# Feed-forward of a hybrid decoder layer: the second product's first raw operands on memory of the first product's last units, loaded by GpSimd's queue

## The chip, the cores and the metric

The kernel runs on one core of one Trainium2 chip. The metric is the device time of one execution in microseconds (us). The core has a tensor engine (TensorE, PE, with its weight loads as PEld), three engines for elementwise work (VectorE or DVE, ScalarE or ACT, GpSimd or POOL), and queues through which transfers between HBM and the on-chip memory are issued. In this kernel nearly all transfers are issued by SyncE (SP), a few by GpSimd.

## The reference

The layer computes attention and a state-space branch, merges them, and then runs a dense feed-forward network. Only the last part matters here:

```python
h = h + merged @ w_out[i]
hn = rmsnorm(h, norm_ffn[i])
gate, up = jnp.split(hn @ w_ffn_in[i], 2, axis=-1)
h = h + (jax.nn.silu(gate) * up) @ w_ffn_out[i]
return h[:, N_META:]
```

`h` is 1024 x 1024 in float32, `w_ffn_in` is 1024 x 5632 and `w_ffn_out` 2816 x 1024.

## The kernel before

All large products are exact to float32: each operand is split into a high and a low part (`hi` by a cast on ScalarE, `lo` by a subtraction on VectorE or GpSimd), and three matmuls (high-high, high-low, low-high, `PASSES`) take the place of one. On top of it the feed-forward network uses a scheme of seven products for a 2 x 2 block product instead of eight. The products are called "11", "12", "2", "3", "1", "22" and "4", in the order in which they run (`ORDER`), and their operands are sums and differences of quarters.

*First product.* For each even j of 0 to 20, `ffn_unit` computes a gate unit `fg{j}` and an up unit `fu{j}`; `fg20` and `fu20` are the last. Their activations' halves are in the X tiles (`Xt..`, `Xb..`), which stay on chip for the whole first product. `finish` (L1163) multiplies silu(gate) by up, makes the sums a1, a2, c12 (the operand "3") and a4 on GpSimd, and stores the seven results to `act_d` in HBM by SP (L1179).

*Second product.* `ffn_out(j0, n, last)` runs four times, with (j0, n) = (0,2), (2,3), (5,3), (8,3). Each stage loads seven raw A operands of `act_d` (`rawa`, L1206; 512 KB each where n is 2) and two raw weight tiles of `w_ffn_out` (`rawb`, L1211; 1 MB each where n is 2). `rawb0_0` holds b11 and b12, `rawb0_1` b21 and b22. VectorE makes t1 = b12 - b11, t2 = b22 - t1, t3 = b22 - b12 and t4 = b21 - t2, which are the B operands of products "1", "2", "3" and "22". `operand` (L1225) splits: the high half on ScalarE (L1228), the low half on VectorE for A and on GpSimd for B (L911, a helper that all elementwise sums share). Each product has four groups (one per row block b) of n x 3 matmuls of 128x128 by 128x512: 24 matmuls where n is 2, 36 where n is 3. The results are in PSUM banks `ch` and `si`; VectorE adds each of them to the residual tiles `h2o0` to `h2o7` (L911). `h2o` is loaded once, in stage j0=0, by 16 loads of 256 KB (L1198). Products "11", "2", "1", "4" share the banks `ch`, so product "2" can only write a bank after VectorE has added it to h2o.

*What sets the order.* Every engine and every queue runs its instructions in order. The order itself is set by a scheduler when the program is built, from its own model of the times, and instructions wait for each other by semaphores. Tiles come from pools; two tiles that lie on the same memory make the later one's writer wait for the earlier one's last reader. Before, the raw tiles lie where the X tiles were, so SP's first raw load (`rawa11_0`) waits for the last matmul of product "4" of `fu20`, and all loads behind it wait too.

Of the kernel before, what the change touches and what calls it, by code (L numbers as in the profile page):

```python
# [8 lines left out]
F32 = mybir.dt.float32  # L9
F32R = mybir.dt.float32r  # L10
# [7 lines left out]
P = 128  # L18
# [28 lines left out]
def hybrid_layer_kernel(ctx: ExitStack, tc: tile.TileContext, x, meta_tokens, norm_mix, w_in, q_norm, k_norm,  # L47
                        attn_sinks, lam_re, lam_im, log_dt, ssm_b_re, ssm_b_im, ssm_c_re, ssm_c_im, ssm_d,
                        w_glu, attn_branch_norm, ssm_branch_norm, w_out, norm_ffn, w_ffn_in, w_ffn_out, out):
    nc = tc.nc  # L50
    x, out = x[0], out[0]
    w_in, w_glu, w_out, w_ffn_in, w_ffn_out = w_in[0], w_glu[0], w_out[0], w_ffn_in[0], w_ffn_out[0]

    def sbuf(name, bufs, side="left"):
        return tc.tile_pool(name=name, bufs=bufs, side=side, reuse_waits="tile")
# [15 lines left out]
    pool_w = front.enter_context(sbuf("pool_w", 8))  # L71
    pool_r = front.enter_context(sbuf("pool_r", 2))
# [156 lines left out]
    with sbuf("p1", 2) as p1:  # L229
# [147 lines left out]
        fr, fi, den, nr = sm("fr"), sm("fi"), sm("den"), sm("nr")  # L377
# [542 lines left out]
    def parts_of(t):  # L920
        return [t[:, p].rearrange("p (k n) -> p k n", k=4) for p in range(2)]

    early = {}
    with sbuf("op", 2) as op_:
# [32 lines left out]
                    nc.tensor.transpose(pt[:, k * P:(k + 1) * P], v[:, k * P:(k + 1) * P], ident)  # L957
                split(*(X[key][p][:, :, c:c + P] for p in range(2)), pt.rearrange("p (k n) -> p k n", k=4))

        for key in ("b11", "b21", "b22"):  # L960
            x_part(key, pool_x)
        for n in range(2):
            w = w_cols(w_out, n * 512, 512, f"o{n}", nc.vector)
# [115 lines left out]
        mixed("t4", "b21", "t2", ALU.subtract)  # L1079
    big_cm.__exit__(None, None, None)  # L1080

    with sbuf("fp", 2) as fp:
        turn_w = [0]

        def operand(src, name):

            turn_w[0] += 1
            pool = fp if turn_w[0] % 3 == 0 else pool_w
            t = parts_of(pool.tile([P, 2, 512], F32R, tag="w", **({"bufs": 4} if pool is fp else {}), name=name))
            split(*t, src)  # L1090
            return t

# [26 lines left out]
        def ffn_unit(c0, u, name):  # L1119


            a = w_quarters(c0, [(pool_r, fp)[u % 2]] * 2, name)
            ops = {}

            def s_(key, x_, y_, op):
                t = fp.tile([P, 512], F32, tag="sum", name=f"s{key}_{name}")
                t = t.rearrange("p (k n) -> p k n", k=4)
                tt_(t, x_, y_, op)
                return t
            ops["11"] = operand(a["11"], f"w11_{name}")  # L1130
            ops["12"] = operand(a["12"], f"w12_{name}")
            s1 = s_("1", a["21"], a["22"], ALU.add)
            s2 = s_("2", s1, a["11"], ALU.subtract)
            ops["2"] = operand(s2, f"w2_{name}")
            ops["1"] = operand(s1, f"w1_{name}")
            ops["4"] = operand(s_("4", a["12"], s2, ALU.subtract), f"w4_{name}")
            ops["3"] = operand(s_("3", a["11"], a["21"], ALU.subtract), f"w3_{name}")
            ops["22"] = operand(a["22"], f"w22_{name}")

            chain, side, third = bank(f"ch_{name}", "m"), bank(f"si_{name}", "s"), bank(f"th_{name}", "x")  # L1140
            banks[u] = {"11": chain, "12": side, "2": chain, "3": third, "1": chain, "22": third, "4": chain}
            c = {}
            for key in ORDER:
                step_(u, ops, key, key in FIRST, name)
                if key == "11":
                    c["11"] = cell(f"c11_{name}")
                    nc.scalar.copy(c["11"], chain)
                elif key == "12":
                    tt_(c["11"], c["11"], side, ALU.add)
                elif key == "2":  # L1150
                    c["21"] = cell(f"c21_{name}")
                    nc.scalar.copy(c["21"], chain)
                elif key == "3":
                    c["22"] = cell(f"c22_{name}")
                    nc.scalar.copy(c["22"], third)
                elif key == "1":
                    tt_(c["22"], c["22"], chain, ALU.add)
                elif key == "22":
                    tt_(c["21"], c["21"], third, ALU.add)
            c["12"] = chain  # L1160
            return c
# [21 lines left out]
                     [ffn_unit(i * DFF + j * P, j + i, f"f{'gu'[i]}{j}") for i in range(2)]), j)  # L1183


    front.close()
    with (sbuf("fo", 16) as fo, sbuf("rw", 2) as rw, sbuf("ra", 4) as ra, sbuf("fh", 8) as fh,
          sbuf("fs", 3) as fs):
        h2 = [fh.tile([P, D], F32, tag="h", name=f"h2o{b}") for b in range(8)]
        QUARTER = {q: (int(q[0]) - 1, int(q[1]) - 1) for q in ("11", "12", "21", "22")}  # L1190
# [3 lines left out]
        def load_h2(q):  # L1194
            r, cc = QUARTER[q]
            for b in range(4 * r, 4 * r + 4):
                cols = slice(512 * cc, 512 * cc + 512)
                nc.sync.dma_start(out=h2[b][:, cols], in_=h2_d[b][:, cols])  # L1198

        def ffn_out(j0, n, last):  # L1200
# [2 lines left out]

            def load_a(q):
                t = ra.tile([P, G, 512], F32, tag="raw", name=f"rawa{q}_{j0}")[:, :n]
                nc.sync.dma_start(out=t, in_=act_d[q][j0:j0 + n].rearrange("j p n -> p j n"))  # L1206
                raw["a" + q] = t

            def load_b(i):
                t = rw.tile([P, G, D], F32, tag="raw", name=f"rawb{j0}_{i}")[:, :n]  # L1210
                nc.sync.dma_start(out=t, in_=w2[i][:, j0:j0 + n, :])  # L1211
                for h in range(2):
                    raw[f"b{i + 1}{h + 1}"] = t[:, :, 512 * h:512 * h + 512]
            for i, q in enumerate(("11", "12", "2", "1", "3", "22", "4")):
                load_a(q)
                if i < 2:
                    load_b(i)
                if not j0 and i < 4:
                    load_h2(("11", "21", "22", "12")[i])

            def s_(key, x_, y_, op):
                t = fs.tile([P, G, 512], F32, tag="sum", name=f"{key}_{j0}")[:, :n]
# [73 lines left out]
```

## Time and profile before

| | us |
|---|---|
| median of 3 runs | 1692.15 (1691.48 to 1692.57) |
| the profiled execution's own time | 1697.95 |
| its span, first to last instruction | 1696.2 |
| TensorE matmuls busy | 1586.7 (94% of the span) |
| VectorE busy | 1181.0 (70%) |
| ScalarE busy | 695.7 (41%) |
| GpSimd busy | 372.4 (22%) |
| mean granted TensorE clock | 0.975 of full speed |

All times of rows are counted from the start of the span. The feed-forward part begins near 1030 us, its first product ends at about 1463 us, and the second one runs from there to the end at about 1692 us. The profiled execution is longer than the median of the unprofiled runs, so differences are worked out within it and then set against the median.

A row of a timeline gives the start, the duration, the engine, the line, the operation, the tiles written and read (numbers left out), how many instructions are merged, and in brackets how long the engine was idle before and what ended that. A merged row has the idle time of its first instruction only.

### The profile page before, as it was taken

To read this page: it belongs to the slowest core of one execution; us is meant where nothing else is said; L and a number is where in the kernel's file an instruction comes from. 1 tells how busy PE (TensorE), PEld (TensorE's weight loads), DVE (VectorE), ACT (ScalarE), POOL (GpSimd) and SP (SyncE) were. 2 spreads that over 40 slices of the span, in tenths; PEclk is the share of its full clock that TensorE was granted. 3 is DMA by queue.
4 is the path that set the end of the run, shared out by engine and by line. 5 is a ranking of instruction groups with operands and counts; after the bars stand their busy time and mean duration, and the time that the engine had idled before them with its cause. 6 is when DMAs were issued, how large, how long until landed. Compare 5 with 4: busy or idle time off the path is not lost.

```text
span 1696.2 us, 22168 instructions
## 1 busy us (share of the span) xinstructions
PE 1586.7 (94%) x8002; PEld 1318.3 (78%) x8002; DVE 1181.0 (70%) x2280; ACT 695.7 (41%) x1363; POOL 372.4 (22%) x277
## 2 busy tenths in 40 slices
PE   7999888989989999799998897999999999799999
PEld 5788768778867888788887785788888888678787
DVE  7779885999995798732217688865656665399763
ACT  4433425878885421442212333533333333243230
POOL 0000112243321001113323200111111121265441
PEclk9999989999999999999999997999999999999999
DMA  5254442011012874742213341423223331584431
GB/s 190 61 130 133 134 143 74 24 38 45 20 51 60 311 218 131 212 130 75 74 51 104 111 163 57 143 87 106 94 94 116 107 106 56 199 305 159 147 109 75
DMA packets 175359, 196.93 MB, mean 116 GB/s; under 512 B 12769, under 2 KB 125409, under 8 KB 175121
## 3 DMA queue, kind: packets, MB, share of 16 engines
q1 hardware_dynamic: 166736, 183.94, 33.6%
q10 hardware_dynamic: 8288, 11.01, 2.1%
q8 instruction: 63, 1.03, 0.3%
q0 software_dynamic: 224, 0.56, 0.1%
q14 instruction: 48, 0.39, 0.1%
HBM read 140.62 MB, written 54.85 MB: 115 GB/s over the span
## 4 chain that ended last, share of the span: by engine, by line
PE 59%; DVE 14%; DMA 4%; ACT 3%; issue 3%; SPq 0%; POOL 0%; ACTq 0%; DVEq 0%
PE ch_fg L907 6%; PE ch_fu L907 6%; PE ch L907 6%; PE za L122 5%; PE wo L122 5%; PE zb L122 5%; PE si L907 4%; PE g L122 3%; PE th_fg L907 3%; PE th_fu L907 3%; PE q L122 2%; PE si_fg L907 2%; PE si_fu L907 2%; DVE pr L663 1%; DVE cm L207 1%
## 5 line engine op out<-in xcount | busy, mean ns | idle before, releaser
L122 PE MATMUL g<-xn,wh_g 128*128 128x512 f32 x512 | 165.4, 403 | 0.1
L907 PE MATMUL ch<-B,A 128*128 128x512 f32 x528 | 127.2, 398 | 13.8 <-ACT B L1228 7.4
L907 PEld LDWEIGHTS ch<-B,A 128*128 128x128 f32 x528 | 100.7, 192 | 37.7 <-ACT B L1228 7.8
L122 PEld LDWEIGHTS g<-xn,wh_g 128*128 128x128 f32 x512 | 97.2, 192 | 22.7 <-PE s L661 0.3
L122 PE MATMUL q<-wh_q,xn 128*128 128x256 f32 x512 | 105.3, 293 | 5.4 <-ACT qp L620 5.4
L122 PE MATMUL g<-xn,wl_g 128*128 128x512 f32 x256 | 102.2, 399 | 0.0
L907 PE MATMUL si<-B,A 128*128 128x512 f32 x396 | 92.6, 389 | 0.5 <-DVE h2o L911 0.5
L122 PE MATMUL wo<-wh_o,mt 128*128 128x512 f32 x256 | 83.9, 406 | 9.3 <-DVE h L984 4.9
L122 PE MATMUL u<-xn,wh_u 128*128 128x272 f32 (+2 forms) x384 | 92.4, 334 | 0.0
L122 PEld LDWEIGHTS q<-wh_q,xn 128*128 128x128 f32 x512 | 85.1, 196 | 7.0 <-ACT qp L620 5.8
L907 PEld LDWEIGHTS si<-B,A 128*128 128x128 f32 x396 | 74.3, 188 | 16.3 <-issue 0.9
L911 POOL TENSOR_TENSOR a<-c,c_fg 128x512 f32<-128x512 f32 x10 | 15.9, 1586 | 315.0 <-DVE c L911 211.1
L858 DVE TENSOR_TENSOR ssm<-za,zs 128x512 f32<-128x512 f32 x16 | 11.0, 690 | 105.3 <-ACT zs L857 105.3
L1228 ACT CAST A<-rawa 128x1536 fp32r<-128x1536 f32 (+1 forms) x28 | 38.5, 1374 | 99.7 <-issue 49.4
L122 PE MATMUL zb<-zt,wh_zb 128*128 128x512 f32 x256 | 79.3, 390 | 0.0
L122 PE MATMUL za<-zt,wh_za 128*128 128x512 f32 x256 | 79.2, 390 | 0.0
L122 PE MATMUL q<-wl_q,xn 128*128 128x256 f32 x256 | 74.5, 291 | 0.0
L911 DVE TENSOR_TENSOR A<-rawa,A 128x1536 fp32r<-128x1536 f32 (+1 forms) x28 | 65.4, 2334 | 12.5 <-ACT A L1228 12.5
L911 POOL TENSOR_TENSOR B<-t,B 128x1536 fp32r<-128x1536 f32 (+1 forms) x16 | 60.2, 3774 | 54.5 <-ACT B L1228 54.5
L669 ACT ACTIVATE pr<-pr,mn 128x272 f32<-128x272 f32 (+1 forms) x128 | 64.8, 507 | 16.5 <-DVE mn L663 14.0
L122 PEld LDWEIGHTS u<-xn,wh_u 128*128 128x128 f32 x384 | 66.7, 198 | 5.5
L122 PEld LDWEIGHTS wo<-wh_o,mt 128*128 128x128 f32 x256 | 50.0, 196 | 20.5 <-DVE h L984 5.3
(426 smaller groups left out, 4211.6 us busy)
## 6 DMA issues: line engine op xcount, KB each, us to landing
rawa<-act_d SPq DMA_DIRECT2D x21, 768.0 KB
raw_fg<-in_w_ffn_in_dram SPq DMA_DIRECT2D x20, 512.0 KB
raw_fu<-in_w_ffn_in_dram SPq DMA_DIRECT2D x20, 512.0 KB
rawb<-in_w_ffn_out_dram SPq DMA_DIRECT2D x6, 1536.0 KB
act_d<-a SPq DMA_DIRECT2D x33, 256.0 KB
raw_g<-in_w_in_dram SPq DMA_DIRECT2D x16, 512.0 KB
act_d<-c_fg SPq DMA_DIRECT2D x30, 256.0 KB
u_d<-uf SPq DMA_DIRECT2D x64, 65.0 KB
```

The costliest lines, as they stand in the source:

```text
L122: nc.tensor.matmul(o, lhs(kb, a), rhs(kb, b), start=(kb == 0 and i == 0), stop=(kb == n - 1 and i == 2))
L207: nc.vector.tensor_tensor(out=m, in0=v, in1=a[:, 2 * k:2 * k + 2, g0:g0 + 4].unsqueeze(3) .to_broadcast([P, 2, 4, n]), op=ALU.mult)
L663: nc.vector.tensor_tensor_reduce(out=pr[:, h, :n], in0=o[:, :n], in1=mask, scale=1.0, scalar=nsink[:, kv * 4 + h:kv * 4 + h + 1], op0=ALU. ...
L669: nc.scalar.activation(out=pr[:, h, :n], in_=pr[:, h, :n], func=AF.Exp, scale=-1.0, bias=mn[:, h:h + 1], accum_out=den[:, h:h + 1])
L858: nc.vector.tensor_tensor(out=dst, in0=oa, in1=sg, op=ALU.mult)
L907: nc.tensor.matmul(o, lhs(kb, a), rhs(kb, b), start=(first and kb == 0 and i == 0), stop=(kb == n - 1 and i == 2), skip_group_check=not first)
L911: eng.tensor_tensor(out=out, in0=in0, in1=in1, op=op)
L1228: nc.scalar.copy(hi, src)
```

## The change

The pool of the first product that held raw loads, sums, split weights and results is divided into three (`fr`, `fw`, `fp`), the order in which three X parts are allocated changes, and the pools of the second product are laid out in another order: `fh` (the h2o tiles) now stands before `rw` (rawb) and `ra` (rawa). This moves the raw tiles of stage j0=0 to other memory. The nine raw loads of that stage are issued by GpSimd in place of SP, and the 16 loads of h2o are all written behind the raw loads rather than between them.

```diff
-        for key in ("b11", "b21", "b22"):
+        for key in ("b22", "b11", "b21"):
             x_part(key, pool_x)
...
-    with sbuf("fp", 2) as fp:
+
+    with sbuf("fr", 2) as fr, sbuf("fw", 4) as fw, sbuf("fp", 2) as fp:
...
-            pool = fp if turn_w[0] % 3 == 0 else pool_w
-            t = parts_of(pool.tile([P, 2, 512], F32R, tag="w", **({"bufs": 4} if pool is fp else {}), name=name))
+            t = parts_of((pool_w if turn_w[0] % 3 else fw).tile([P, 2, 512], F32R, tag="w", name=name))
...
-            a = w_quarters(c0, [(pool_r, fp)[u % 2]] * 2, name)
+            a = w_quarters(c0, [(pool_r, fr)[u % 2]] * 2, name)
...
-                t = fp.tile([P, 512], F32, tag="sum", name=f"s{key}_{name}")
+                t = fr.tile([P, 512], F32, tag="sum", name=f"s{key}_{name}")
...
-    with (sbuf("fo", 16) as fo, sbuf("rw", 2) as rw, sbuf("ra", 4) as ra, sbuf("fh", 8) as fh,
+    with (sbuf("fo", 16) as fo, sbuf("fh", 8) as fh, sbuf("rw", 2) as rw, sbuf("ra", 4) as ra,
           sbuf("fs", 3) as fs):
...
-                nc.sync.dma_start(out=t, in_=act_d[q][j0:j0 + n].rearrange("j p n -> p j n"))
+                (nc.sync if j0 else nc.gpsimd).dma_start(out=t, in_=act_d[q][j0:j0 + n].rearrange("j p n -> p j n"))
...
-                nc.sync.dma_start(out=t, in_=w2[i][:, j0:j0 + n, :])
+
+                (nc.sync if j0 else nc.gpsimd).dma_start(out=t, in_=w2[i][:, j0:j0 + n, :])
...
-                if not j0 and i < 4:
-                    load_h2(("11", "21", "22", "12")[i])
+
+            if not j0:
+                for q in ("11", "21", "22", "12"):
+                    load_h2(q)
```

In the built program (bytes within a partition) `rawb0_0` now lies on 150,336 to 158,528, and the X tile `Xb220` on 144,192 to 152,384. The load of `rawa11_0` waits for the last matmul of product "11" of `fu20` and for a split on VectorE; the load of `rawb0_0` waits for the last matmul of product "4" of `fu20`, which reads `Xb220`.

GpSimd between the last sums of `fu18` and the second product: before, it has the four sums of `fu20` (a1, a2, c12, a4) and then the low halves of B11, B12 and B2 (the "1" at the end of `B11_01` is the low half).

```order
L911 TENSOR_TENSOR a4_18_12726<-c21_fg18_12532,a2_18_12725 128x512
L911 TENSOR_TENSOR a1_20_13005<-c12_20_13002,c22_fg20_12827 128x512
L911 TENSOR_TENSOR a2_20_13006<-a1_20_13005,c11_fg20_12786 128x512
L911 TENSOR_TENSOR c12_20_13002<-c11_fg20_12786,c12_20_13002 128x512
L911 TENSOR_TENSOR a4_20_13007<-c21_fg20_12813,a2_20_13006 128x512
L911 TENSOR_TENSOR B11_01_13086<-rawb0_0_13049,B11_00_13085 128x1024
L911 TENSOR_TENSOR B12_01_13094<-rawb0_1_13057,B12_00_13093 128x1024
```

The same place of GpSimd after:

```order
L1207 DMA rawa11_0_13055<-act11_d_80 128x2x512
L1213 DMA rawb0_0_13057<-in_w_ffn_out_dram 128x2x1024
L1207 DMA rawa12_0_13059<-act12_d_81 128x2x512
L1213 DMA rawb0_1_13061<-in_w_ffn_out_dram 128x2x1024
L1207 DMA rawa2_0_13063<-act2_d_82 128x2x512
L1207 DMA rawa1_0_13065<-act1_d_84 128x2x512
L911 TENSOR_TENSOR a1_20_13011<-c12_20_13008,c22_fg20_12833 128x512
L1207 DMA rawa3_0_13067<-act3_d_83 128x2x512
L911 TENSOR_TENSOR a2_20_13012<-a1_20_13011,c11_fg20_12792 128x512
L911 TENSOR_TENSOR c12_20_13008<-c11_fg20_12792,c12_20_13008 128x512
L911 TENSOR_TENSOR B11_01_13094<-rawb0_0_13057,B11_00_13093 128x1024
L911 TENSOR_TENSOR a4_20_13013<-c21_fg20_12819,a2_20_13012 128x512
```

Six loads stand ahead of the sums now, a seventh between the first two, and a4 has moved behind the low half of B11. On SP the 16 loads of h2o come up to the place of the raw loads, ahead of the stores of a1, a2, c12 and a4.

VectorE behind the last sum of the first product, before: the low halves of A11, A12 and A2, then t1, t2, t3, then the adds of product "11" (`ch0_..`) and "12" (`si120_..`) to h2o.

```order
L911 TENSOR_TENSOR A11_01_13082<-rawa11_0_13047,A11_00_13081 128x1024
L911 TENSOR_TENSOR A12_01_13090<-rawa12_0_13055,A12_00_13089 128x1024
L911 TENSOR_TENSOR A2_01_13102<-rawa2_0_13063,A2_00_13101 128x1024
L911 TENSOR_TENSOR t1_0_13097<-rawb0_0_13049 128x1024
L911 TENSOR_TENSOR t2_0_13099<-rawb0_1_13057,t1_0_13097 128x1024
L911 TENSOR_TENSOR t3_0_13117<-rawb0_1_13057,rawb0_0_13049 128x1024
L911 TENSOR_TENSOR h2o0_13039<-h2o0_13039,ch0_0_13145 128x512
L911 TENSOR_TENSOR h2o1_13040<-h2o1_13040,ch0_1_13146 128x512
L911 TENSOR_TENSOR h2o0_13039<-h2o0_13039,si120_0_13177 128x512
```

The same place after:

```order
L911 TENSOR_TENSOR h2o0_13047<-h2o0_13047,ch0_0_13153 128x512
L911 TENSOR_TENSOR h2o1_13048<-h2o1_13048,ch0_1_13154 128x512
L911 TENSOR_TENSOR h2o2_13049<-h2o2_13049,ch0_2_13155 128x512
L911 TENSOR_TENSOR A2_01_13110<-rawa2_0_13063,A2_00_13109 128x1024
L911 TENSOR_TENSOR h2o3_13050<-h2o3_13050,ch0_3_13156 128x512
L911 TENSOR_TENSOR h2o0_13047<-h2o0_13047,si120_0_13185 128x512
L911 TENSOR_TENSOR h2o1_13048<-h2o1_13048,si120_1_13193 128x512
L911 TENSOR_TENSOR h2o2_13049<-h2o2_13049,si120_2_13201 128x512
L911 TENSOR_TENSOR h2o3_13050<-h2o3_13050,si120_3_13209 128x512
L911 TENSOR_TENSOR t1_0_13105<-rawb0_0_13057 128x1024
L911 TENSOR_TENSOR t2_0_13107<-rawb0_1_13061,t1_0_13105 128x1024
L911 TENSOR_TENSOR t3_0_13125<-rawb0_1_13061,rawb0_0_13057 128x1024
```

All eight adds of products "11" and "12" stand ahead of t1, t2 and t3 now; the low halves of A11 and A12 stand just ahead of this piece, as before. On TensorE the seven products of stage j0=0 keep their order; at the start of stage j0=2 the first two of four groups of product "12" have moved ahead of the first group of product "11". From stage j0=5 on the orders of all engines are the same. At the start of unit j=2 of the first product a few raw loads and splits have changed places.

## Rows read from the trace of the kernel before

**Rows 1.** Timeline of PE around the change: start us, us, engine, line, tiles, [idle before]

```profile
1460.21 2.88 PE L907 MATMUL ch_fu<-Xb,w_fu 128*128 128x512 f32 x12
1470.52 2.08 PE L907 MATMUL ch<-B,A 128*128 128x512 f32 x4 [7.42 <-ACT B L1228]
1472.96 5.53 PE L907 MATMUL ch<-B,A 128*128 128x512 f32 x20 [0.37 <-POOL B L911]
1478.33 5.60 PE L907 MATMUL si<-B,A 128*128 128x512 f32 x24
1484.90 0.47 PE L907 MATMUL ch<-B,A 128*128 128x512 f32 x1 [0.96 <-DVE h2o L911]
1485.57 4.15 PE L907 MATMUL ch<-B,A 128*128 128x512 f32 x17 [0.20 <-DVE h2o L911]
```

**Rows 2.** Timeline of SP's queue, same columns

```profile
1463.12 0.37 SPq L1206 DMA_DIRECT2D rawa<-act_d  x1
1463.59 0.42 SPq L1211 DMA_DIRECT2D rawb<-in_w_ffn_out_dram  x1
...
1501.08 0.37 SPq L1211 DMA_DIRECT2D rawb<-in_w_ffn_out_dram  x1
```

**Rows 3.** Timeline of ScalarE (ACT)

```profile
1469.42 1.04 ACT L1228 CAST B<-rawb 128x1024 fp32r<-128x1024 f32 x1 [1.58 <-DMA rawb<-in_w_ffn_out_dram]
...
1480.45 1.06 ACT L1228 CAST B<-t 128x1024 fp32r<-128x1024 f32 x1 [4.54 <-DVE t L911]
```

**Rows 4.** Timeline of GpSimd (POOL)

```profile
1464.01 1.26 POOL L911 TENSOR_TENSOR a<-c,c_fg 128x512 f32<-128x512 f32 x1 [27.48 <-DVE c L911]
...
1470.54 2.37 POOL L911 TENSOR_TENSOR B<-rawb,B 128x1024 fp32r<-128x1024 f32 x1 [1.49 <-ACT B L1228]
1474.54 2.40 POOL L911 TENSOR_TENSOR B<-rawb,B 128x1024 fp32r<-128x1024 f32 x1 [1.63 <-ACT B L1228]
1481.59 8.09 POOL L911 TENSOR_TENSOR B<-t,B 128x1024 fp32r<-128x1024 f32 x3 [4.64 <-ACT B L1228]
```

**Rows 5.** Stretches: length, busy us of each engine, clock, DMA share, GB/s

```profile
1478.00:1485.00 7.00, 6.04 (x28) 4.71 (x26) 4.38 (x6) 4.55 (x5) 3.41 (x2) 1.00 1.05 401
1515.00:1535.00 20.00, 20.00 (x90) 16.57 (x89) 20.00 (x12) 8.58 (x6) 14.33 (x4) 1.00 0.54 187
```

**Rows 6.** Timeline of VectorE (DVE)

```profile
1477.95 1.21 DVE L911 TENSOR_TENSOR t<-rawb 128x1024 f32<-128x1024 f32 x1
...
1484.06 1.45 DVE L911 TENSOR_TENSOR h2o<-h2o,ch 128x512 f32<-128x512 f32 x2 [2.51 <-DMA h2o<-h_d]
...
1544.02 2.47 DVE L911 TENSOR_TENSOR h2o<-h2o,ch 128x512 f32<-128x512 f32 x4
...
1559.49 1.76 DVE L911 TENSOR_TENSOR t<-rawb,t 128x1536 f32<-128x1536 f32 x1 [3.08 <-DMA rawb<-in_w_ffn_out_dram]
...
1575.47 2.47 DVE L911 TENSOR_TENSOR h2o<-h2o,ch 128x512 f32<-128x512 f32 x4
```

**Rows 7.** Timeline of PE from j0=2 to j0=5

```profile
1514.41 8.41 PE L907 MATMUL ch<-B,A 128*128 128x512 f32 x36 [1.37 <-DVE h2o L911]
...
1531.04 8.10 PE L907 MATMUL ch<-B,A 128*128 128x512 f32 x35
...
1563.45 8.32 PE L907 MATMUL ch<-B,A 128*128 128x512 f32 x36
1572.24 0.47 PE L907 MATMUL si<-B,A 128*128 128x512 f32 x1 [0.46 <-DVE h2o L911]
1576.20 10.08 PE L907 MATMUL ch<-B,A 128*128 128x512 f32 x36 [3.49 <-DVE h2o L911]
```

**Rows 8.** GpSimd's issue early in the program, and its transfers (KB, us to landing)

```profile
48.48 0.60 POOL L434 DMA_DIRECT2D kl_d<-zrows  x1 [0.29 <-POOL zrows L433]
...
kl_d<-zrows POOLq DMA_DIRECT2D x1, 448.0 KB, 3.5
...
lt<-in_lam_re_dram POOLq DMA_DIRECT2D x1, 32.0 KB, 6.7
```

## The prediction, made before the changed kernel was run

> **What bounds the kernel now.** TensorE (PE) is busy for 94% of the span, so I read its row of the timeline first and looked for the places where it stands still. Around the change there are two. The first feed-forward product ends at 1463.09, and the second begins only at 1470.52, after 7.42 us of waiting for ScalarE's cast of B [rows 1]. Later, at the border from stage j0=2 to j0=5, PE waits 0.46 and then 3.49 us for VectorE's adds to h2o [rows 7].
>
> The next view is the queue of SyncE (SP). Its first raw load goes out at 1463.12, the moment the last matmul ends [rows 1, 2], and the first weight tile rawb at 1463.59 [rows 2]. ScalarE casts B at 1469.42, once rawb has landed [rows 3]. GpSimd makes the last four sums meanwhile, then the low half of B11 until 1472.91 [rows 4]; only then do the other 20 matmuls of product "11" run. The memory is the limit in this stretch: between 1478 and 1485 the DMA engines are 1.05 busy at 401 GB/s [rows 5]. VectorE waits 2.51 us for the first h2o load at 1484.06 [rows 6], and from then it is a bound beside PE: it is busy for all 20.00 us of 1515 to 1535 [rows 5].
>
> **The change, part by part.** *The early load.* The new places let rawa11 go about 20 us early. But rawb0_0 lies on 150,336 to 158,528 and the last Xb operand on 144,192 to 152,384: 2,048 bytes in common, and in the built program its issue waits for the very last matmul of unit fu20. On GpSimd's queue everything behind it waits too. So of the seven operands' loads only one, 512 KB, moves ahead; the cast of A11 and its low half go ahead with it, but B is what PE waited for [rows 1, 3]. I cost this at nothing.
>
> *rawb0_0 on GpSimd's queue.* It goes out at about 1463.2. Landing, lower bound: on SP's queue rawa11 and rawb0_0 were in 6.3 us after 1463.12 [rows 2, 3], 1.5 MB, of which 3.8 are moving at 400 GB/s [rows 5], so 2.5 are fixed; with 1 MB (2.6) this gives 1463.2 + 0.6 + 2.5 + 2.6 = 1468.9. (0.60 us is what GpSimd's queue took to issue 448 KB, which landed after 3.5 us, so a transfer by that queue needn't be slow [rows 8].) Upper bound: all 16 h2 loads (4.2 MB) now start on SP's queue at the same moment, which halves the share: 1471.5; and the 32 KB lt load by GpSimd took 6.7 us [rows 8], which would make it up to 4 us later still, 1475. I take 1470.5, nearer to the 448 KB row, since its kind (wide, mid-program) is nearer.
>
> *GpSimd itself.* Ahead of B11's low half it now has five issues (5 x 0.6 = 3.0), three sums (3.8) and one more issue (0.6) from 1463.2: free at 1470.6. B11's low half starts at 1471.5 (landing plus 1.04 for the cast) and ends at 1473.9: +0.9 (bounds 0 and +5.6).
>
> *Product "12".* rawb0_1 is third in that queue, with 2.6 MB behind 1463.2 by then: landing between 1471.6 (whole rate) and 1478 (half). GpSimd does a4 and one issue (1.9) between the two low halves, then 2.40 [rows 4]: B12 is ready between 1478.2 and 1481.4, against PE's need at about 1480.3. So I add 0.6, and "12" ends at 1485.4 instead of 1483.9: +1.5 (bounds 0 and +6.8).
>
> *VectorE's order.* This is the largest term. Before, t1, t2 and t3 (1.21 each) ran from 1477.95 on, under product "12" [rows 1, 6]. Now eight h2o adds stand ahead of them, and the last of these waits for the last matmul of "12". Product "2" needs B2 = t2, so behind the end of "12" come in a row: an add (0.62, a quarter of the 2.47 for four), t1 and t2 (2.4) [rows 6], the cast (1.06) [rows 3], and the hand-overs (0.3): 4.4 us until PE's four high-high matmuls, and then the rest of B2's low half (2.6 each of the three in 8.09 [rows 4], less 0.9): 6.1 us of idle PE. Before, 0.96 + 0.20 stood there [rows 1]. +4.9.
>
> *Clock.* After the gap of 3.49 us the next 36 matmuls took 10.08 us, against 8.16 for others [rows 7]. The new gap is in two pieces; I take +1.0 (bounds 0 and 1.9).
>
> *Border of j0=0 to j0=2.* PE's 1.37 us of waiting for h2o [rows 7] goes: product "12" of the next stage now has two of its groups ahead of the chain that waits. In exchange B12 of j0=2 is needed early. Its rawb2_1 is issued when B4's low half frees the tile, 1501.08 before [rows 2], and some 3.5 us later now; it is ready about when PE comes (0 to 1.5 us late, I take 0.2). -1.2.
>
> So at the start of j0=2 PE is late by 1.5 + 4.9 + 1.0 - 1.2 = +6.2 us; I call this lateness S.
>
> *What the later wait gives back.* At the border to j0=5 PE stood 3.95 us for VectorE, and lost 1.9 more to the lower clock: 5.85 [rows 7]. Whether VectorE is late as well decides. Its own work: t1 now starts at 1486.2, and 3.6 us of t come back into its row, while eight adds (0.62 each, 5.0) have been done before: 1486.2 + 3.6 - 5.0 against 1484.06 is +0.8. It then runs without idle time, so PE's lateness is met by its backlog: the four adds of j0=2's product "2" end at 1546.5 [rows 6], while PE had finished that product at 1539.1 [rows 7], which leaves more than 6 us. I add 1.1 for two places where it must wait for PE. The wait for rawb5_1 at 1559.49 [rows 6] moves with the low half of A4, so by the same 1.9. VectorE's first add of the last product then comes at 1577.4 instead of 1575.47 [rows 6], and PE can go on at 1578.1. PE itself ends stage j0=2 at 1571.75 + 6.2 = 1577.95. The two meet: PE resumes 1.9 us later than at 1576.20, without a gap long enough for the lower clock (the gap of 1.37 us had none), which gives 1.9 back. Net 0, and by S - 5.85 with S = 6.2, +0.35. As the bounds of S reach further up than down, +0.8.
>
> From j0=5 on all engines have the same order, PE without a gap. The few loads and splits that change places at the start of unit j=2 I cost at nothing, since their products run under those of the unit before.
>
> **Sum.** The profiled execution took 1697.95 (span 1696.2), 5.8 more than the median of 1692.15; I expect 1698.8 for it and 1693.0 for the median.
>
> **Rivals.**
> 1. *Slower: two queues share the engines.* If GpSimd's loads get half the rate, or its descriptors come as slowly as with lt, rawb0_0 lands at 1475 and rawb0_1 at 1482.7. Then "12" ends near 1490.7 (+6.8), S = 6.8 + 4.9 + 1.5 - 1.2 = 12, and 12 - 5.85 = +6: 1698. It decides as soon as "12" ends after about 1488.5 (S over 9.2). For it: 1.05 busy engines [rows 5] and 4.2 MB of h2 moved ahead of need. Against: GpSimd's 448 KB in 3.5 us. Chance 0.23. The Trainium skill, "DMA: Bandwidth & Descriptors", section "Queues, rings and completion order", says that each DMA engine goes round-robin between the queues that hold work for it; by that rule the half rate would hold until h2 is in, and this rival is the likelier. No row here has both queues at work.
> 2. *Slower: nothing is given back.* If VectorE's wait for rawb5_1 moves by all of S, since the casts ahead of it wait for operand tiles that PE frees, the 3.95 us stay: +6.2, 1698.3. For it: that row's releaser is a DMA. Against: VectorE's full 20.00 us. Chance 0.12.
> 3. *Faster, by VectorE.* With h2 there at 1470, VectorE's adds start some 5 us sooner. If it keeps that lead through j0=2, in which it never idles [rows 5], it comes to j0=5 before 1575, and if the bubble at t2 is only 3 us, PE at 1574: -2 and -1.9 for the clock, 1688.3. Chance 0.08.
> 4. *The change does what its title says*: rawb0_0 lands before 1463. Then "11" starts about 4 us earlier, S is +2, VectorE -2: also about 1688. The common 2,048 bytes speak against. Chance 0.04.
>
> **Numbers.** The forecast (within 0.2%, that is 3.4 us, about what a measurement of this kernel can tell from no change) has 0.53. Faster by more: rivals 3 and 4, 0.12. Slower by more: rivals 1 and 2, 0.35. The range leaves out half of rivals 3 and 4 and the upper half of 1 and 2: 1689 to 1699.
>
> **What would show it.** Right: one raw load near 1443 and the next at 1463 on GpSimd's queue; PE starting "11" at 1470 to 1473; t2 behind the end of "12", with an idle PE of 4 to 7 us there at about 1486 to 1493; j0=2 starting near 1520.6; and nearly no gap at the start of j0=5. Wrong: a rawb landed before 1463, no gap ahead of product "2", or j0=5 starting after 1582 (then it is rival 1 or 2, told apart by whether VectorE or PE is the later one there).

## The result, and the profile after

The changed kernel takes 1702.99 us (median of 4 runs, 1702.21 to 1704.21) against 1692.01 beside it (1691.48 to 1692.57): ratio 1.0066, interval 1.0048 to 1.0083. It is slower by 0.66%, and lies above the forecast of 1693.0 and above the upper end of the range, 1699. Its profiled execution took 1703.57, its span is 1701.8.

The two profiled executions don't end the first product at the same time: the last matmul of `fu20` ends at 1462.13 in after and at 1463.09 in before [rows 1]. So below I count from that matmul's end. Counted so, the rest of the program takes 233.1 us before and 239.7 after: +6.6. That is the part behind the change; what lies ahead of it comes at the end of the next section.

Timeline of TensorE in after (start us, us, engine, line, tiles, count, [idle before]), which answers to [rows 1, 7]:

```profile
1459.25 2.88 PE L907 MATMUL ch_fu<-Xb,w_fu 128*128 128x512 f32 x12
1471.88 2.08 PE L907 MATMUL ch<-B,A 128*128 128x512 f32 x4 [9.75 <-ACT B L1232]
1474.32 5.94 PE L907 MATMUL ch<-B,A 128*128 128x512 f32 x20 [0.36 <-POOL B L911]
1480.10 5.60 PE L907 MATMUL si<-B,A 128*128 128x512 f32 x24
1490.01 1.77 PE L907 MATMUL ch<-B,A 128*128 128x512 f32 x4 [4.31 <-ACT B L1232]
1492.47 7.05 PE L907 MATMUL ch<-B,A 128*128 128x512 f32 x20 [0.69 <-POOL B L911]
...
1524.29 3.89 PE L907 MATMUL si<-B,A 128*128 128x512 f32 x14 [1.67 <-POOL B L911]
...
1574.68 8.32 PE L907 MATMUL ch<-B,A 128*128 128x512 f32 x36
...
1583.38 8.46 PE L907 MATMUL ch<-B,A 128*128 128x512 f32 x36
```

Four things are to be read here. The wait ahead of "11" has grown from 7.42 to 9.75. Ahead of "2" stands a new gap of 4.31 + 0.69, and the last 20 matmuls of "2" take 7.05, while 18 take 4.24 elsewhere in this trace (from 1506.84). At j0=2 there is a wait of 1.67 for a low half of B. And at j0=5 (1583.38) there is no gap: the 3.49 of before [rows 7] is gone.

VectorE, SyncE's queue and GpSimd at the same place, which answer to [rows 6, 2, 4]:

```profile
1485.74 0.69 DVE L911 TENSOR_TENSOR h2o<-h2o,si 128x512 f32<-128x512 f32 x1 [0.45 <-PE si L907]
1486.35 1.22 DVE L911 TENSOR_TENSOR t<-rawb 128x1024 f32<-128x1024 f32 x1
1487.65 1.23 DVE L911 TENSOR_TENSOR t<-rawb,t 128x1024 f32<-128x1024 f32 x1
1491.74 1.76 DVE L911 TENSOR_TENSOR t<-rawb,rawb 128x1024 f32<-128x1024 f32 x1 [2.86 <-DMA act_d<-a]
```

```profile
1461.32 17.39 SPq L1199 DMA_DIRECT2D h2o<-h_d  x16
1480.47 2.35 SPq L1179 DMA_DIRECT2D act_d<-a  x2
...
1485.26 0.32 SPq L1179 DMA_DIRECT2D act_d<-a  x1
```

```profile
1462.44 0.74 POOL L1213 DMA_DIRECT2D rawb<-in_w_ffn_out_dram  x1 [24.92 <-PE ch_fu L907]
...
1471.90 2.36 POOL L911 TENSOR_TENSOR B<-rawb,B 128x1024 fp32r<-128x1024 f32 x1 [1.39 <-ACT B L1232]
1474.23 2.26 POOL L911 TENSOR_TENSOR a<-c_fg,a 128x512 f32<-128x512 f32 x1
...
1477.86 2.40 POOL L911 TENSOR_TENSOR B<-rawb,B 128x1024 fp32r<-128x1024 f32 x1 [0.70 <-ACT B L1232]
```

t1 starts only behind the last add of "12" (1485.74), as the prediction had it. What it had not seen is in t3's row: it waits 2.86 for a store. t3 lies on the memory of the sum a4, which GpSimd had made by 1476.49, and a4's store goes out at 1485.26, since the 16 h2o loads stand ahead of it on SP. The four stores do not only come behind the issues of these loads: each of them waits for an earlier h2o load to land (5.3 us in all).

The clock behind the gap ahead of "2", and at the same place before (columns: stretch, length, busy PE, PEld, DVE, ACT, POOL, granted clock, DMA share, GB/s; after first):

```profile
1490.40:1497.20 6.80, 6.11 (x15) 4.33 (x14) 5.46 (x3) 4.39 (x5) 6.80 (x3) 0.50 0.42 144
```

```profile
1485.60:1492.40 6.80, 6.80 (x29) 5.38 (x30) 6.80 (x9) 0.65 (x1) 4.08 (x2) 1.00 1.05 387
```

0.50 is the lower of the two levels, 1.2 GHz: in 6.80 us 15 matmuls instead of 29. It came behind the idle time ahead of "2".

### The profile page after: what moved, and what is told of

Its sections match the earlier page's. It is cut to its first block, busy times and chain, and to the rows that moved or that the text cites. A ratio compares the mean times of both kernels' runs of the same rounds, so it can differ in the third digit from the quotient of the medians.

```text
span 1701.8 us, 22178 instructions
## 1 busy us (share of the span) xinstructions
PE 1591.0 (93%) x8002; PEld 1321.2 (78%) x8002; DVE 1178.2 (69%) x2280; ACT 695.6 (41%) x1363; POOL 377.4 (22%) x286
## 4 chain that ended last, share of the span: by engine, by line
PE 55%; DVE 18%; DMA 5%; ACT 3%; issue 3%; SPq 0%; ACTq 0%; DVEq 0%
PE ch_fg L907 6%; PE ch_fu L907 6%; PE za L122 5%; PE wo L122 5%; PE zb L122 5%; PE ch L907 4%; PE g L122 3%; PE th_fg L907 3%; PE th_fu L907 3%; PE si L907 3%; PE q L122 2%; DVE A L911 2%; PE si_fg L907 2%; PE si_fu L907 2%; DVE pr L663 2%
## 5 line engine op out<-in xcount | busy, mean ns | idle before, releaser
L907 PEld LDWEIGHTS si<-B,A 128*128 128x128 f32 x396 | 74.1, 188 | 18.5 <-POOL B L911 2.1
L911 POOL TENSOR_TENSOR a<-c,c_fg 128x512 f32<-128x512 f32 x10 | 15.9, 1587 | 287.7 <-DVE c L911 183.6
L911 DVE TENSOR_TENSOR A<-rawa,A 128x1536 fp32r<-128x1536 f32 (+1 forms) x28 | 61.5, 2199 | 14.8 <-ACT A L1232 14.8
```

Of the source, the lines that this page charges most:

```text
L907: nc.tensor.matmul(o, lhs(kb, a), rhs(kb, b), start=(first and kb == 0 and i == 0), stop=(kb == n - 1 and i == 2), skip_group_check=not first)
L911: eng.tensor_tensor(out=out, in0=in0, in1=in1, op=op)
```

## The experiments

For each run I counted the matmuls behind the last one of `fu20` and subtracted, for four of them, the time in before's trace from the time in the run's: "12" is the end of the 48th, j0=0 that of the 168th, S the end of the 420th (the end of stage j0=2), and the end is that of the span. All in us. "S less end" is what a version got back, or lost, between the end of j0=2 and the end.

| run | edit | "12" | j0=0 | S | end | S less end | ratio to before (95%) |
|---|---|---|---|---|---|---|---|
| after | | +2.7 | +10.3 | +12.2 | +6.6 | 5.6 | 1.0066 (1.0048 to 1.0083) |
| e0 | before again | +1.5 | +0.2 | +0.2 | +0.1 | 0.1 | 0.9997 (0.9979 to 1.0015) |
| e4 | after again | +2.4 | +10.0 | +11.8 | +6.2 | 5.6 | 1.0057 (1.0037 to 1.0076) |
| e1 | t's first | +2.1 | +13.8 | +15.9 | +9.8 | 6.1 | 1.0080 (1.0057 to 1.0102) |
| e2 | h2o late | -0.7 | +3.9 | +4.7 | -0.3 | 5.0 | 1.0011 (0.9995 to 1.0026) |
| e9 | h2o late, t's first | -0.5 | +6.0 | +5.7 | +0.3 | 5.3 | 1.0013 (0.9999 to 1.0027) |
| e3 | rawb apart | +1.6 | +11.6 | +13.5 | +8.0 | 5.5 | 1.0055 (1.0036 to 1.0074) |
| e10 | e9 and rawb apart | -1.4 | +3.5 | +4.2 | -1.3 | 5.5 | 1.0011 (0.9997 to 1.0025) |
| e5 | stores by GpSimd | +3.2 | +10.3 | +18.5 | +12.3 | 6.2 | one run, 1709.09 us |
| e6 | e5 and t's first | +2.4 | +9.6 | +15.1 | +8.8 | 6.3 | 1.0074 (1.0051 to 1.0096) |
| e7 | all early | -5.9 | -0.1 | -1.7 | -0.6 | -1.1 | 0.9984 (0.9968 to 1.0000) |
| e8 | raw loads by SP | +1.7 | +8.2 | +14.0 | +7.9 | 6.1 | 1.0065 (1.0045 to 1.0086) |
| e11 | before, raw loads by GpSimd | +3.5 | +9.4 | +9.4 | +3.8 | 5.6 | 1.0035 (1.0019 to 1.0052) |

**e0, e4: the two kernels again.** 

> The kernel before, unchanged, profiled again. Theory A (the wait of 3.95 us at the border of j0=2 to j0=5, with 1.9 us of lower clock behind it, belonged to the one profiled execution of before and not to its usual runs: together 5.85, and that execution took 5.80 more than the median): no gap over 1 us at the start of j0=5, span near 1690.5. Rival B (the gap belongs to the program, and the profile costs some 6 us elsewhere): the gap of 3 to 4 us stands there again, span near 1696.

> The changed kernel again, beside the others on one chip. From the end of the first product (the last matmul of fu20) to the end of the span the kernel before took 233.1 and 233.4 us in its two profiles, the changed one 239.7. Theory A (all the change costs lies behind the first product, and what else parts the medians is the part ahead of it, which differs from execution to execution by some 6 us): this stretch takes 239.4 to 240.0 again, and the median is 6 to 8 us over that of before on the same chip. Rival B (the first part is slower as well): the median is 10 or more over that of before, with the gap of 3.5 us near 1031 to 1036 coming later than in the profiles of before.

In e0 the gap ahead of j0=5 stands again, with the slow 36 matmuls behind it:

```profile
1570.98 10.04 PE L907 MATMUL ch<-B,A 128*128 128x512 f32 x36 [3.50 <-DVE h2o L911]
```

So it belongs to before, though the span is 1690.9, where theory A had it. The 5.4 us between the two profiled executions of before lie ahead of the change: `fu20` ends at 1463.09 in one and 1457.69 in the other, and behind it they differ by 0.1. e4 repeats after, gaps and all, behind `fu20`; its median is 10.2 us over that of before, as rival B had it and not the 6 to 8 of theory A.

**e1: t1 to t3 ahead of the adds** (`t3_ins` is the instruction that makes t3).

```diff
+                if q == "11" and not j0:
+                    with tc.issue_after(t3_ins):
+                        tt_(dst, dst, o, ALU.add)
```

> The changed kernel, with VectorE's eight adds of products 11 and 12 of stage j0=0 queued behind t1, t2, t3; loads and queues as in the changed kernel. Theory A (VectorE's order is the largest part of the loss): the idle time ahead of product 2 falls from 4.31 + 0.69 us to under 1.5, the lower clock behind it (20 matmuls in 7.05 us) goes, and the time falls by 6 to 8, to 1695 to 1697. Rival B (the late landing of rawb and of the stores sets it): product 12 still ends at 1485.7, t2 waits for rawb0_1 and the time falls by under 3, to 1700 or more.

It got slower. t1 and t2 come 5.5 us earlier, but t3 can't, and now all adds stand behind it; PE waits for the first of them 8.65 us (VectorE, then PE):

```profile
1482.13 1.23 DVE L911 TENSOR_TENSOR t<-rawb,t 128x1024 f32<-128x1024 f32 x1
1491.75 1.22 DVE L911 TENSOR_TENSOR t<-rawb,rawb 128x1024 f32<-128x1024 f32 x1 [8.39 <-DMA act_d<-a]
```

```profile
1493.71 6.58 PE L907 MATMUL ch<-B,A 128*128 128x512 f32 x15 [8.65 <-DVE h2o L911]
```

So VectorE's order is not the whole bubble: the late store limits t3, whatever stands ahead.

**e2: the h2o loads behind the last four stores on SP.**

```diff
+                if q == "4":
+                    last_store[0] = nc.cur_bb.bb.instructions[-1]
...
+                with tc.issue_after(last_store[0]):
+                    nc.sync.dma_start(out=h2[b][:, cols], in_=h2_d[b][:, cols])
```

> The changed kernel, with the 16 h2o loads queued on SP behind the four last stores of the first product, so that they start after 1475 instead of 1461; VectorE's order follows: t1 ahead of the adds, t2 and t3 behind the first of them. Theory A (the two queues share the DMA engines and the raw loads pay): rawb0_0 lands 1.5 to 3 us sooner than 8.3 us after its issue, rawb0_1 4 to 5 us sooner than 12.8, t3 doesn't wait for the store of a4 any more; the time is 1692 to 1695. Rival B (the landing is set by GpSimd's own way of issuing): rawb0_0 lands 8 us after its issue as before, and product 11 starts no earlier; only the order on VectorE helps, 1696 to 1698.

The loss behind `fu20` goes: end -0.3 instead of +6.6. rawb0_0 lands 4.9 us after its issue and rawb0_1 7.8, against 8.3 and 12.8 in after, so the raw loads do pay for the sharing, as theory A had it. PE waits 6.36 ahead of "11" (after: 9.75), and the gap ahead of "2" is shorter. VectorE's order changes with this edit (t1 ahead of the adds, t2 and t3 behind the first), so the run does not part the two:

```profile
1466.51 2.08 PE L907 MATMUL ch<-B,A 128*128 128x512 f32 x4 [6.36 <-ACT B L1236]
...
1483.60 0.50 PE L907 MATMUL ch<-B,A 128*128 128x512 f32 x1 [3.27 <-ACT B L1236]
1484.85 7.29 PE L907 MATMUL ch<-B,A 128*128 128x512 f32 x23 [0.75 <-DVE h2o L911]
```

**e9: e2 and e1 together.** 

> The changed kernel with both edits: the 16 h2o loads behind the last four stores on SP, and the eight adds of "11" and "12" behind t3 on VectorE. With the first edit alone the stretch was 232.9 us, with 3.3 + 0.75 us of PE's wait ahead of product "2" and 1.6 at j0=2; with the second alone 243.0, since t3 waited 8.4 us for a store. Theory 1 (t3 waits only because the stores stand behind h2o): t3 does not wait for act_d, the gap ahead of "2" shrinks to under 2 us, S falls to about 0 to 2. Then theory B (VectorE bounds the later border to j0=5) says the wait of about 3.5 us comes back there and the stretch stays 232 to 233.5; theory A (the wait there is an accident of the order) says the gain stays, stretch 229 to 231. Rival to theory 1 (VectorE's new order itself costs): the gap ahead of "2" stays over 5 us and the stretch is over 237.

t3 waits for no store now, and still nothing is gained: the adds wait for h2o, which comes late, and PE for the adds, in three pieces:

```profile
1482.40 0.47 PE L907 MATMUL ch<-B,A 128*128 128x512 f32 x1 [2.16 <-DVE h2o L911]
1484.63 0.49 PE L907 MATMUL ch<-B,A 128*128 128x512 f32 x1 [1.75 <-DVE h2o L911]
1486.31 7.85 PE L907 MATMUL ch<-B,A 128*128 128x512 f32 x22 [1.18 <-DVE h2o L911]
```

S is 5.7 where I expected 0 to 2, so the step on the gap was wrong; the end, +0.3, is where the bound by VectorE puts it.

**e3, e10: rawb on memory that is free.** 2,048 unused bytes a partition stand ahead of rawb, so that rawb0_0 shares nothing with the last Xb operand (one element of them is written, on VectorE behind t3).

```diff
-    with (sbuf("fo", 16) as fo, sbuf("fh", 8) as fh, sbuf("rw", 2) as rw, sbuf("ra", 4) as ra,
+    with (sbuf("fo", 16) as fo, sbuf("fh", 8) as fh, sbuf("fx", 1) as fx, sbuf("rw", 2) as rw, sbuf("ra", 4) as ra,
```

> The changed kernel, with 2,048 unused bytes between the h2o tiles and the rawb tiles, so that rawb0_0 no longer touches the X tile of the last matmuls; the rest of the order is the same. Theory A (the 2,048 bytes are why PE still waits): rawb0_0 goes out near 1437, PE waits under 2 us between the products, product 12 then waits for rawb0_1, whose landing comes some 4 us sooner (1472): it ends near 1480, and as VectorE's order is unchanged the bubble behind it stays: 1696 to 1698. Rival B (rawb0_1's landing at 1476.7 does not move, as the h2o loads take what is freed): product 12 ends at 1485 as before and the time stays at 1701 to 1703.

> As the run with both edits, and 2,048 unused bytes a partition ahead of rawb, so that rawb0_0 can be loaded some 20 us before the first product ends, but with GpSimd's sums and loads in the changed kernel's order. With the pad alone PE started "11" at once, waited 8.7 us for the low half of B11, which stood behind loads and sums in GpSimd's queue, and lost 8.5 us ahead of "2" again: stretch 241.2. Theory 1: the wait of 8.7 us stays (the early load alone gives nothing) and the gap ahead of "2" goes; stretch 231.5 to 234, not below the run without the pad by more than 1 us. Rival (the early load is worth its 4 us once the stores no longer wait): stretch 228 to 230.

In e3 PE starts "11" at once, does four matmuls and waits 8.65 for the low half of B11, which stands behind issues and sums in GpSimd's row (PE, then POOL):

```profile
1462.21 0.50 PE L907 MATMUL ch<-B,A 128*128 128x512 f32 x1 [0.16 <-DVE c L911]
1471.37 7.00 PE L907 MATMUL ch<-B,A 128*128 128x512 f32 x20 [8.65 <-POOL B L911]
```

```profile
1467.75 1.27 POOL L911 TENSOR_TENSOR c<-c_fg,c 128x512 f32<-128x512 f32 x1
1468.98 2.34 POOL L911 TENSOR_TENSOR B<-rawb,B 128x1024 fp32r<-128x1024 f32 x1
```

The pad also moved t1 onto a sum's tile; the end is +8.0. The time, 1702.8, is where rival B put it, but not for its reason: rawb0_1's cast starts at 1472.12 (after: 1476.71), and the gap ahead of "2" has grown to 8.49. With the edits of e9 the end is -1.3 (e10), 1.6 less than without the pad, a little more than I expected; PE waits 6.22 for the low half of B11, and a gap of 4.40 ahead of "2" stays, where I expected none. In both runs t1 waits some 3 to 4 us for a store, so the pad is not the early load alone.

**e5, e6: the last stores by GpSimd, behind their sums.**

```diff
-                nc.sync.dma_start(out=act_d[q][j // 2], in_=t)
+                (nc.gpsimd if j == NFF - 2 and len(q) == 1 else nc.sync).dma_start(out=act_d[q][j // 2], in_=t)
```

> The changed kernel, with the last four stores of the first product (a1, a2, c12 and a4 of unit 20) issued by GpSimd right behind the sums, no longer by SP behind the 16 h2o loads; VectorE's order is as in the changed kernel. Theory A (adds ahead of t2 make the bubble): the idle time ahead of product 2 stays at 4 to 5 us, though t3 no longer waits for a store, and the stretch behind the first product takes 238 to 240. Rival B (the late stores, whose tiles lie where t1 to t4 go, make the loss): the stretch falls to 236 or less.

> The same with VectorE's eight adds behind t1, t2, t3 as well, which with the late stores waited 8.4 us at t3. Theory A (order and stores together are the loss, sharing the DMA engines only some 2 us of it): no idle time over 2 us ahead of product 2, the stretch behind the first product takes 233.5 to 235.5, the time is 1694 to 1696. Rival B (the h2o loads' share of the DMA engines is the loss): product 2 starts no earlier than 4 us behind the end of product 12, the stretch takes 237 or more.

Theory A misses in both. In e5 t3 waits no longer, but t1 and t2 stand behind "12" as in after, the gap ahead of "2" stays (4.31 + 0.39), and the stretch is 245.3, over what either theory had: VectorE's work of j0=2 now stands so that PE waits there again:

```profile
1525.87 1.19 PE L907 MATMUL si<-B,A 128*128 128x512 f32 x2 [3.62 <-DVE h2o L911]
1530.09 4.88 PE L907 MATMUL si<-B,A 128*128 128x512 f32 x11 [3.03 <-DVE A L911]
```

In e6, with t1 to t3 first, t3 waits 5.13 for a store all the same: on GpSimd's queue the stores land behind the raw loads' bytes, which share the DMA engines with h2o (a4's store took 11.7 us to land). Its numbers are those of rival B: "2" starts 5.73 behind "12", and the stretch is 241.8.

**e7: everything early.** The pad, both rawb loads ahead of rawa12, the low halves of B11 and B12 ahead of the last sums, h2o behind the stores, the adds of "11" and "12" behind t3. 

> A version that does what the title says: 2,048 unused bytes ahead of rawb, rawb0_0 and rawb0_1 both issued ahead of rawa12, the low halves of B11 and B12 ahead of the last sums on GpSimd, the h2o loads behind the last stores on SP, and the adds behind t3 on VectorE. Theory A (what early operands save is PE's wait between the products, and the wait for VectorE at the start of j0=5 takes part of it back): product 11 starts within 1 us of the first product's end, product 12 within 2.5 us of the end of 11, and the stretch takes 228 to 231: 1688 to 1692. Rival B (VectorE and the DMA engines are the bound from here to j0=5): PE is early at product 11 and waits as much more later, mostly at the starts of j0=2 and j0=5, so that the stretch takes 232.5 or more and the time is that of before.

PE has no wait ahead of "11" and ends "12" 5.9 us earlier. But VectorE can't follow (t1 waits 3.16 for a store, the adds come behind it), and at j0=5 the old gap is back, as rival B had it (stretch 232.5):

```profile
1461.59 2.00 PE L907 MATMUL ch<-B,A 128*128 128x512 f32 x8
...
1481.33 7.14 PE L907 MATMUL ch<-B,A 128*128 128x512 f32 x18 [4.65 <-DVE h2o L911]
...
1569.18 0.47 PE L907 MATMUL si<-B,A 128*128 128x512 f32 x1 [0.45 <-DVE h2o L911]
1573.15 7.03 PE L907 MATMUL ch<-B,A 128*128 128x512 f32 x18 [3.50 <-DVE h2o L911]
```

Its median is 1688.07, the lowest of all; the interval of the ratio reaches 1.0000, so it is not shown to beat before.

**e8, e11: each half of the change alone.** e8 is after with the raw loads issued by SP; e11 is before with them issued by GpSimd:

```diff
-                nc.sync.dma_start(out=t, in_=w2[i][:, j0:j0 + n, :])
+                (nc.sync if j0 else nc.gpsimd).dma_start(out=t, in_=w2[i][:, j0:j0 + n, :])
```

> The changed memory and code order, but the nine raw loads of stage j0=0 issued by SP again, as before. The order then built: on SP the stores of a1, a2, c12 and a4 stand between the first raw loads and the first h2o loads again, on GpSimd the low halves of B11 and B12 stand behind the four sums without loads between, on VectorE t1 to t3 stand behind five to seven of the adds of "11" and "12". The stretch from the last matmul of fu20 to the end of the span is 233.1 us before and 239.7 after. Theory 1 (the loss comes from the h2o loads standing ahead of the stores and beside GpSimd's raw loads): the stores go out by 1470, no t waits for a store, rawb0_0 lands within 6.5 us of the end of the first product; a gap of 3 to 4 us stays ahead of product "2" since t2 still stands behind adds of "12"; stretch 232 to 235, ratio to before 0.999 to 1.002. Rival (the places of the tiles or the order of VectorE alone make the loss): a gap of 6 us or more ahead of "2", stretch 238 to 240, ratio 1.004 to 1.007.

> The kernel before with one edit: the nine raw loads of stage j0=0 are issued by GpSimd; memory and the rest of the code stay. In the built program the four last stores stand ahead of all h2o loads on SP, t1, t2 and t3 stand ahead of all adds on VectorE (as before), and on GpSimd six loads stand ahead of the sums, a2 and c12 behind the low half of B11 and a4 behind that of B12. With the other edit alone (memory and code order, raw loads by SP) the stretch from the last matmul of fu20 to the end was 241.0 us, with both 239.7, before 233.1. Theory 1 (VectorE's order and its wait for stores make the loss, the queue of the raw loads does not): rawb0_0 lands within 6.5 us of the end of the first product, no t waits for a store, the gap ahead of "2" stays under 2.5 us, S at the end of j0=2 is under 4, of which the border to j0=5 gives back all; stretch 232 to 234.5, ratio 0.999 to 1.003. Rival (GpSimd's queue makes a loss of its own, by its issues and the late low halves): S over 8, stretch 237 to 240, ratio 1.003 to 1.006.

I expected both to be harmless, and both lose, e8 +7.9 and e11 +3.8 at the end; in e11 it is the rival that came, with S at 9.4. In e8 the stores go out between the first loads and no t waits for one, but t1 and t2 stand behind adds of "12", as in after:

```profile
1487.72 2.07 PE L907 MATMUL ch<-B,A 128*128 128x512 f32 x4 [3.65 <-ACT B L1232]
...
1524.97 7.08 PE L907 MATMUL ch<-B,A 128*128 128x512 f32 x18 [3.43 <-DVE h2o L911]
```

In e11 VectorE has the order of before. There GpSimd is late: a4 comes behind eight issues and the low halves of B11 and B12 (1477.24), its store behind it, and only then, at 1479.95, the h2o loads; the first add waits for h2o until 1485.62 (POOL, SP, DVE, PE):

```profile
1477.24 2.27 POOL L911 TENSOR_TENSOR a<-c_fg,a 128x512 f32<-128x512 f32 x1
```

```profile
1479.95 10.66 SPq L1198 DMA_DIRECT2D h2o<-h_d  x16
```

```profile
1485.62 2.03 DVE L911 TENSOR_TENSOR h2o<-h2o,ch 128x512 f32<-128x512 f32 x3 [3.90 <-DMA h2o<-h_d]
```

```profile
1467.97 2.07 PE L907 MATMUL ch<-B,A 128*128 128x512 f32 x4 [10.16 <-ACT B L1228]
...
1486.46 8.97 PE L907 MATMUL ch<-B,A 128*128 128x512 f32 x24 [4.30 <-ACT A L1228]
```

**What follows.** The loss has two sources, and the losses of e8 and e11 do not add up to that of after. GpSimd's queue makes the last sums and low halves late, and with them the stores; behind the stores h2o is late (e11), ahead of them h2o holds them and takes rate from the raw loads (after against e2). And the order built with the new memory puts t1 and t2 behind the adds of "12" (after, e8); no run has the new memory, SP's queue and the old order, so that it is this order in e8, and not the places of the tiles, is argued and not shown. Only where h2o stands behind the stores and rawa11 is early does S fall to 6 or less (e2, e9, e10: 4 to 6; e7: -1.7), and the 4 to 6 are given back whole. The column "S less end" says why no version wins more: of a PE that is late, 5.0 to 6.3 us are taken up at j0=5, where PE waited for VectorE before (eleven traces); a PE that is early waits there (e7).

**What stays open.** The medians differ by more than the traces behind `fu20`: 0.66% is 11 us, the traces show 6.6; for e2 1.9 and -0.3; for e7 -2.7 and -0.6. The first product is not where the rest lies: from its first matmul into an `fg` tile to the end of `fu20` all fourteen traces take 384.6 to 384.8 us. The differences are there when the feed-forward begins. The wait of 3.5 us that ends at 1036.6 in before ends at 1031.1 in e0, at 1031.4 in e11, and between 1033.5 and 1036.3 in the eleven traces with the new memory, though up to there the engines run the same instructions in the same order in after and e0, by the names of their tiles. Whether the new memory keeps that part late, or these executions happened to be, was not tried.

## Why the prediction was wrong, point by point

Times of after are given as in before's profile, that is +0.96.

- **The early load, costed at nothing.** Which load moves was right: one raw load early (rawa11), rawb0_0 only behind the last matmul. "Nothing" was wrong where h2o is out of the way: with rawa11 early (at 1436.72, 25.7 us ahead of rawb0_0) PE waits 6.36 ahead of "11" (e2), without it 10.16 (e11), on the same queue with no h2o beside it. Not all of the 3.8 is the load's: e11's queue also began slower (last section), and the 512 KB alone are, as an estimate, 1.3 us at e2's 396 GB/s. In after the gain is lost again to h2o.
- **rawb0_0's landing.** Forecast 1470.5, measured 1471.7 (the cast starts at 1470.78): in the bounds. GpSimd's issues took 0.72 each, not 0.60, but B11's low half waited for the cast in the end (1.39); it ended 2.3 late, not 0.9. **"12"** ended 2.7 late, not 1.5, in the bounds; 1486.7, so rival 1's point of decision for it, 1488.5, was not reached.
- **VectorE's order.** The step was right in kind and nearly in size: the wait for B2's cast was forecast at 4.4 and is 4.31. Idle PE between "12" and the end of j0=0 grew by 4.4 (4.31 + 0.69 + 0.39 + 0.17, less 0.96 + 0.20 [rows 1]) against 4.9. (Of that, 2.6 for a low half is a slip: 8.09 over three is 2.7.) The wait of t3 for a store was missed altogether. In after it moves t3 and what is behind it; e1 shows its price when t1 and t2 are on time, 8.39 us.
- **Clock: the term that was mis-sized.** Forecast +1.0 with an upper bound of 1.9. From "12" to the end of j0=0 PE lost 7.6, 4.4 of it idle; the other 3.2 are the clock: the 4 and 20 matmuls behind the gap took 1.77 and 7.05, where 4 take 1.07 elsewhere in this trace and 20, by the 4.24 of 18 and 0.23 for each more, 4.7: 3.1 of it. I sized it by a gap of 3.49 [rows 7] and then halved it because the new gap is in two pieces; rows give no reason for the halving. Nor was the whole enough: behind the gap of 3.49 the granted clock was 0.50 from 1576.9 to 1580.2 and then 1.00, in after it was 0.50 for all of the 6.8 us shown above. Why the low stretch is longer the runs don't show. Before:

```profile
1576.90:1580.20 3.30, 3.30 (x10) 2.53 (x9) 3.30 (x3) 0.00 (x0) 1.98 (x1) 0.50 0.60 226
1580.30:1586.00 5.70, 5.70 (x27) 4.68 (x26) 3.20 (x5) 0.00 (x0) 0.00 (x0) 1.00 0.43 141
```

- **Border to j0=2: the sign was wrong.** Forecast -1.2, measured +1.9 (S 12.2 less 10.3). The 1.37 of before did go, but B12's low half came 1.67 late and not 0.2, and three shorter waits behind it (the longest 0.38) make up most of the rest. The step that failed is rawb2_1: I had it issued 3.5 us after 1501.08 [rows 2], as soon as B4's low half frees its tile, and it went out at 1511.01 (1512.0 in before's time). B4's low half, which stands behind those of B3 and B22 in GpSimd's row, ended at 1509.43, and on SP a load of A stands ahead of rawb2_1 that waited until 1510.52 for VectorE's low half of A4 (SP, then VectorE). The prediction followed GpSimd alone. How much of the delay is t3's wait and how much the gap ahead of "2" was not separated.

```profile
1496.85 14.04 SPq L1207 DMA_DIRECT2D rawa<-act_d  x4
1511.01 0.42 SPq L1213 DMA_DIRECT2D rawb<-in_w_ffn_out_dram  x1
```

```profile
1508.27 2.24 DVE L911 TENSOR_TENSOR A<-rawa,A 128x1024 fp32r<-128x1024 f32 x1
```

- **S** was 12.2, not 6.2: +1.2 by "12", +2.2 by the clock, +3.1 at the border, -0.5 by the idle time. So the two terms that failed are the border and the clock.
- **What the later wait gives back.** Right: 5.6 against 5.85. (The 1.9 in it sets 10.08 against 8.16, which leaves out the overlap with the next matmul; against 8.32 [rows 7] it is 1.8.) It held in nine other versions with S from 4.2 to 18.5, and S less 5.85 would have given +6.4 for the measured S, against 6.6.
- **Rival 1** has the right total, S = 12 and +6, by other terms. Its sharing of the engines is there (below), and e2 gives its price, 3.4 us for rawb0_0 and 5.0 for rawb0_1, but it moved "12" by 2.7 and not by 6.8. Its other signs came: S over 9.2, and j0=5 starting after 1582 (1582.84, that is 1583.8), with PE as the later one there. Rivals 2 to 4 didn't come.
- **From profile to median.** I took 5.8 off, the difference between before's profiled execution and its median. After's profiled execution is within 0.6 of its median. The difference lies ahead of the change and comes and goes with the execution (e0). With the right S the forecast would have been 1692.15 + 6.6 = 1698.7; the other 4 us up to 1703.0 are the part that stays open.

## What to carry to other kernels

Before costing a load that is moved ahead on an in-order queue, list what was ahead of it there, stores too, and whose memory those stores still hold: here 16 loads held back four stores, and a tile of the next stage lay on what they read. Moving loads to an engine that also computes costs that engine's next results first, here 0.72 us an issue. And find the next place where another engine is the bound: it gives back a delay, or swallows a gain, and a sum of the gaps ahead of it says little about the end.

## What the runs showed of the hardware

With two queues at work the DMA engines moved as many packets of the one as of the other, not as many bytes. The page on the queues in after, from 1465 to 1475 (queue, packets, MB, share of 16 engines; q0 is GpSimd's, q1 SP's):

```profile
q0 software_dynamic: 682, 2.63, 67.0%
q1 hardware_dynamic: 689, 1.26, 33.9%
```

The packet counts are equal, GpSimd's packets are about twice as large, and so it got two thirds of the rate. The Trainium skill ("DMA: Bandwidth & Descriptors", "Queues, rings and completion order") says that each DMA engine goes round-robin between the queues by whole packets. The equal counts agree with that, though whether a packet of the profile is what the page calls one, no run here shows. The half rate that rival 1 made of it doesn't follow, since the packets differ in size.

Alone, GpSimd's queue can be as fast as SP's: in e2 it moved 1.59 MB in the 4 us from 1463 to 1467 (396 GB/s), and in e11 SP's alone moved 3.94 MB in the 10 us from 1486 to 1496 (394 GB/s). In e11 GpSimd's queue began slower, with 1.49 MB in the 5 us from 1460 to 1465 (298 GB/s); why, no run shows. GpSimd's in e2, SP's in e11, GpSimd's in e11:

```profile
q0 software_dynamic: 419, 1.59, 102.5%
```

```profile
q1 hardware_dynamic: 2011, 3.94, 104.5%
```

```profile
q0 software_dynamic: 391, 1.49, 85.0%
```
